# Layer 0's second shift computed as row sums on VectorE, with only the second scale left to TensorE

## The chip, the cores and the metric

The kernel runs on 1 core of one Trainium2 chip. A time is the device time of one execution in microseconds (us), lower is better. The core's engines are TensorE (PE in the rows; its weight loads are PEld), VectorE (DVE), ScalarE (ACT), GpSimd (POOL) and SyncE (SP), whose queue starts most DMA transfers. Each engine works through its own instructions in order.

## What is computed

Two layers of a hybrid diffusion backbone are applied to 128 context tokens and 256 latent tokens of width 1024. Each layer has a token-mixing half and a ConvFFN half, and both are modulated by six vectors that come from a conditioning vector. Cut to what matters here:

```python
def layer(x, mod, p, latent, kc, vc):
    sh1, sc1, g1, sh2, sc2, g2 = jnp.split(mod, 6)   # mod = silu(c) @ w_mod + b_mod
    h = layer_norm(x) * (1 + sc1) + sh1
    z = h @ p["w_in"] + p["b_in"]        # q, k, v, conv input, Fourier input, 3 gates
    ...                                  # attention, conv and Fourier branches
    merged = ga * a_attn + gc * a_conv + gf * a_f
    x = layer_norm(ALPHA * x + g1 * (merged @ p["w_o"]))
    h = layer_norm(x) * (1 + sc2) + sh2
    u = dwconv(h @ p["w_up"])
    ug, uv = jnp.split(u, 2)
    x = layer_norm(ALPHA * x + g2 * ((silu(ug) * uv) @ p["w_down"]))
```

There are two conditioning vectors (context and latent), so each of the six vectors exists twice. All inputs are float32.

## The kernel before

Tokens are kept transposed (`hT`: channels on the partitions, 384 tokens along the free axis). A float32 product is made of three matmuls (`mm3`, lines 197 to 200) on a high and a low half of each operand. For each weight tile `halves` (lines 171 to 183) has ScalarE cast the high half (`whi`, L181) and VectorE subtract it for the low half (`wlo`, L182). There are five buffers for each half.

The mixing half of a layer runs three branches one after the other, each over eight output tiles m of 128 channels (`branch`): branch 0 Fourier, branch 1 attention, branch 2 convolution. For a tile, TensorE makes a gate product of 24 matmuls into one of two `ps` accumulators, then the branch's own product into one of six `acc` accumulators (6 matmuls in branches 0 and 2, 12 in branch 1). ScalarE takes the tanh of the gate (L586), VectorE multiplies gate and product (L600), which frees the `acc` accumulator, and GpSimd adds the result to the running sum (L601). In branch 2 the finished sum is split into halves `r` (L569 on ScalarE, L570 on VectorE). Afterwards the output projection with `w_o` begins.

Beside that run, as generators that are stepped once per tile:

- attention: `scores` (softmax) and `values`, which transposes the probabilities and copies them out of the accumulators, 512 columns by ScalarE (L801) and 384 by VectorE (L802), before the products with V (L810, L813). There are 4 calls of `values` for a layer, with 2 copies of each kind.
- the depthwise convolution, 31 taps on VectorE (L828), whose results TensorE transposes (L836) for a layer norm.
- modulation by TensorE: `mod_stream` loads `w_mod` and multiplies it by the two conditioning vectors, which are padded to 32 columns (`cpad`). For each of 8 values of k, four matmuls on four quarters of the array (L219) cover 4 x 512 columns. They make layer 0's second shift and second scale in one go (kind "B"). `mod_columns` then copies the rows (L284), transposes them (L288) and adds the bias (L296).
- modulation by VectorE: `mod_rows` makes one of the six vectors (a unit) as row sums. For each of 8 tiles of `w_modr` (128x1024, two buffers) and each of the two conditioning vectors, one instruction multiplies and sums over 1024 columns (L318). In layer 0's mixing half it makes only the first gate, (0,"G",0). `paced(rows, n)` spreads the steps over n calls.
- `gate_rows`, right after the last tile of branch 2: TensorE transposes the gate's 16 sums (L338), ScalarE copies them and a DMA takes them to memory, from where they are broadcast.

A framework puts each engine's instructions into one fixed order when the program is built. The order is therefore not that of the source alone.

Of the kernel before, what the change touches and what calls it, by code (L numbers as in the profile page):

```python
# [13 lines left out]
ALU = mybir.AluOpType  # L14
AX = mybir.AxisListType

P = 128
D = 1024
KD = D // P
# [58 lines left out]
class Net:  # L78
# [130 lines left out]

    MODS = {"A": 0, "B": 1, "G": 2}  # L210

    STRIDE = 2

    def mod_products(self, ps, src, ks, n):

# [20 lines left out]
        self.mod_columns(l, "A", ps, P, 2 * s, "ps")  # L236
        yield

    def mod_stream(self, groups):


        steps = [(l, kind, k) for l, kind in groups for k in range(0, KD, self.STRIDE)]
        src = {}

        def fetch(l, kind, k0):
            for k in range(k0, k0 + self.STRIDE):
                w = self.a["w_mod"][l, self.MODS[kind], k].rearrange("p j (i c) -> p (j i) c", c=512)
                for i in range(4):
                    src[k, i] = self.s2()
                    self.load(src[k, i], w[:, i])  # L250

        fetch(*steps[0])
        yield
        for n, (l, kind, k0) in enumerate(steps):
            if k0 == 0:
                ps = self.psum("acc")
            self.mod_products(ps, src, range(k0, k0 + self.STRIDE), 512)
            if k0 + self.STRIDE == KD:
                if kind == "G":
                    self.mod_gates(l, ps)  # L260
                else:
                    self.mod_columns(l, kind, ps, 512, 0, "acc")
            if n + 1 < len(steps):
                fetch(*steps[n + 1])
            yield

    def mod_gates(self, l, ps):
        nc, a, n = self.nc, self.a, 512
        row = self.s2()
        nc.gpsimd.memset(row, 0.0)  # L270
        r4 = row.rearrange("(j i r) c -> j i r c", r=32, j=2)
        for v in range(2):
            for j in range(2):
                self.load(r4[j, :, v, :], a["b_g"][l, j].rearrange("(i c) -> i c", c=n))
        nc.vector.tensor_tensor(row, ps, row, op=ALU.add)
        for v in range(2):
            for j in range(2):
                nc.sync.dma_start(self.gscr[l, j, v].rearrange("(i c) -> i c", c=n), r4[j, :, v, :])

    def mod_columns(self, l, kind, ps, n, k0, tag):  # L280

# [259 lines left out]
    def mixing(self, l, first, hT, mods, rows):  # L541
        nc, a = self.nc, self.a
# [4 lines left out]
        def conv_in():  # L547
            gl = []
            for u in range(2):
                for j, w in enumerate(self.halves(self.col_halves(self.raw(a["w_cv"][l, u])))):  # L550
                    ps = self.ws_tile(hT, w)
                    gt = self.g()[:, 0:NTOK]
                    bias = cols["b_conv"][:, 2 * u + j:2 * u + j + 1]
                    if u == 0:
                        nc.scalar.activation(gt, ps, AF.Identity, bias=bias)
                    else:
                        nc.scalar.activation(gt, ps, AF.Tanh, bias=bias, scale=0.5)
                    gl.append(gt)
                    yield
            for j in range(2):  # L560
                for o, s, n in ((UP_S, 0, LAT), (UP_P, LAT, CTX)):
                    nc.vector.scalar_tensor_tensor(self.upad[j][:, o:o + n], gl[2 + j][:, s:s + n], 1.0,
                                                   gl[j][:, s:s + n], op0=ALU.add, op1=ALU.mult)
# [44 lines left out]

        if l + 1 < DEPTH:
            self.columns(l + 1)  # L610
        mods = self.mod_stream(mods) if mods else iter(())

        def mod():
            next(mods, None)

        step_rows = self.paced(rows, 10)
        ci = conv_in()
        next(ci)
        cv = self.keys(l, z)
# [20 lines left out]
                mod()  # L640
        for i, _ in enumerate(branch(1, 0, "w_a", 4, aT, lambda: values(3))):
            next(cb, None)
            if i >= 4:
                step_rows()
            if i % 2:
                mod()
# [84 lines left out]
    def attention(self, l, z, cv, out):  # L731
        nc, a = self.nc, self.a
# [57 lines left out]
        def values(j):  # L790
            pT = []
            for par in range(2):
                pr = prob.pop(2 * j + par)
                pts = [self.psum("acc"), self.psum("acc")]
                for i in range(3):
                    dst = pts[i // 2][:, (i % 2) * 256:(i % 2) * 256 + 256]
                    for t in range(2):
                        nc.tensor.transpose(dst[:, t * P:(t + 1) * P], pr[t][:, i * P:(i + 1) * P], self.ident)  # L798
                nc.tensor.transpose(pts[1][:, 256:384], pr[2], self.ident)
                p = self.s4()  # L800
                nc.scalar.copy(p[:, 0:512], pts[0])  # L801
                nc.vector.tensor_copy(p[:, 512:896], pts[1][:, 0:384])  # L802
                pT.append(p)
            po = self.psum("acc")
            vc = slice(j // 2 * HD, j // 2 * HD + HD)
            for i in range(4):
                for par in range(2):
                    pv = po[64 * par:64 * par + 64, :]
                    if i < 3:
                        nc.tensor.matmul(pv[:, 0:LAT], vs[i][:, vc], pT[par][:, i * 256:i * 256 + 256],  # L810
                                         start=i == 0, stop=i == 2)
                    else:
                        nc.tensor.matmul(pv[:, LAT:NTOK], vs[3][:, vc], pT[par][:, 768:896], start=True, stop=True)  # L813
            out.append(self.split_r(po[:, 0:NTOK]))
# [235 lines left out]
    def run(self):  # L1050
        self.setup()
        xhat = [self.s4() for _ in range(3)]
        for t in range(3):
            self.load(xhat[t], self.x_src(0, t))
        self.columns(0)
        for x in xhat:
            self.norm(x, x, D)
        mods = [[(0, "B")], []]
        mix_rows = [[(0, "G", 0)], [(1, "G", 0)]]
        ffn_rows = [[(0, "G", 1), (1, "A", 0), (1, "A", 1), (1, "B", 0), (1, "B", 1)], [(1, "G", 1)]]  # L1060
        first, hT = xhat, self.new_hT(0)
        for l in range(DEPTH):
            first, hT = self.layer(l, first, hT, mods[l], mix_rows[l], ffn_rows[l])
# [79 lines left out]
```

## Time and profile before

| | us |
|---|---|
| median of 3 runs (1138.2 to 1139.53) | 1138.48 |
| the profiled execution, its own time | 1139.04 |
| its span, from first to last instruction | 1137.3 |
| TensorE busy | 1115.4 |
| VectorE busy | 887.9 |
| ScalarE busy | 520.7 |

The profiled execution was 0.56 us above the median, and 1.74 us of its time lie outside the span. Times in the rows below count from the start of the span. Layer 0's three branches lie between about 90 and 256 us.

### The profile page before, as it was taken

The page shows a single profiled execution, that of the slowest core. Times are in us where ns is not written, and L with a number is a line of the kernel's source. Part 1 is how long each engine was busy: PE and PEld are TensorE (multiplying, and loading weights), DVE is VectorE, ACT ScalarE, POOL GpSimd, SP SyncE. Part 2 cuts the span into 40 slices and gives each one's busy share as a digit, 9 for nine tenths or more (in the row PEclk, how much of TensorE's full clock was granted, in tenths as well). Part 3 has the DMA queues.
Part 4 walks back from the last instruction along what each step waited for, and adds up shares of the span by engine and source line. Part 5 has one row for each costly group of instructions (what it writes and reads, how often), then busy time and mean ns, then how long its engine had stood idle before and what let it go on. Part 6 is the DMA issues. An engine that isn't in the chain of part 4 may idle for free.

```text
span 1137.3 us, 16435 instructions
## 1 busy us (share of the span) xinstructions
PE 1115.4 (98%) x6377; PEld 1013.8 (89%) x6377; DVE 887.9 (78%) x1529; ACT 520.7 (46%) x879; POOL 89.6 (8%) x89
## 2 busy tenths in 40 slices
PE   8999999999999999999999999999999999999996
PEld 6788889998999998999957989999889999999995
DVE  5579977855899999999776699796588975556668
ACT  2447653342753443444363686343356343444440
POOL 1010003221100000000021000222120000000001
PEclk9999999999999999999999999999999999999998
DMA  9753563636466666758324322564627543434511
GB/s 376 293 199 135 175 243 126 202 131 222 165 229 211 229 215 213 236 188 286 121 109 173 110 75 74 186 222 149 222 94 259 190 144 114 147 112 156 178 38 56
DMA packets 41822, 199.04 MB, mean 175 GB/s; under 512 B 4912, under 2 KB 6032, under 8 KB 26640
## 3 DMA queue, kind: packets, MB, share of 16 engines
q1 hardware_dynamic: 41312, 197.21, 49.7%
q8 instruction: 50, 0.82, 0.3%
q10 hardware_dynamic: 432, 0.79, 0.2%
q14 instruction: 28, 0.23, 0.1%
HBM read 194.53 MB, written 3.45 MB: 174 GB/s over the span
## 4 chain that ended last, share of the span: by engine, by line
PE 81%; DVE 10%; DMA 3%; ACT 3%; POOL 1%; issue 1%; SPq 0%; POOLq 0%; DVEq 0%; ACTq 0%
PE ps L198 16%; PE ps L200 16%; PE ps L199 16%; PE acc L199 9%; PE acc L200 9%; PE acc L198 9%; DVE s L318 1%; PE acc L810 1%; DVE wlo L182 1%; DMA s<-w_z 1%; DVE sm L404 1%; ACT whi L181 1%; DVE s L861 1%; POOL sm L408 1%; PE acc L798 1%
## 5 line engine op out<-in xcount | busy, mean ns | idle before, releaser
L182 DVE TENSOR_TENSOR wlo<-raw,whi 128x1024 fp32r<-128x1024 f32 x216 | 269.0, 1249 | 146.5 <-ACT whi L181 146.4
L198 PE MATMUL ps<-hT,whi 128*128 128x386 f32 (+1 forms) x1088 | 370.2, 340 | 2.4 <-ACT g L586 1.4
L181 ACT CAST whi<-raw 128x1024 fp32r<-128x1024 f32 x216 | 225.7, 1049 | 312.6 <-PE ps L199 185.6
L200 PE MATMUL ps<-hT,wlo 128*128 128x386 f32 (+1 forms) x1088 | 368.6, 339 | 0.0
L199 PE MATMUL ps<-hT,whi 128*128 128x386 f32 (+1 forms) x1088 | 368.5, 339 | 0.0
L198 PEld LDWEIGHTS ps<-hT,whi 128*128 128x128 f32 x1088 | 205.1, 189 | 9.4 <-issue 3.9
L199 PEld LDWEIGHTS ps<-hT,whi 128*128 128x128 f32 x1088 | 205.3, 189 | 1.5 <-issue 0.4
L200 PEld LDWEIGHTS ps<-hT,wlo 128*128 128x128 f32 x1088 | 205.2, 189 | 0.8 <-issue 0.7
L318 DVE SCALAR_TENSOR_TENSOR s<-s,s 128x1024 f32<-128x1024 f32 x128 | 160.6, 1255 | 4.4 <-DMA s<-w_modr 3.9
L199 PE MATMUL acc<-wlo,r 128*128 128x512 f32 x360 | 142.3, 395 | 1.0 <-DVE wlo L182 1.0
L200 PE MATMUL acc<-whi,r 128*128 128x512 f32 x360 | 141.9, 394 | 0.0
L198 PE MATMUL acc<-whi,r 128*128 128x512 f32 x360 | 140.3, 395 | 0.0
L200 PEld LDWEIGHTS acc<-whi,r 128*128 128x128 f32 x360 | 67.6, 188 | 15.9 <-DVE r L994 0.5
L199 PEld LDWEIGHTS acc<-wlo,r 128*128 128x128 f32 x360 | 67.6, 188 | 15.6 <-DVE wlo L182 1.3
L198 PEld LDWEIGHTS acc<-whi,r 128*128 128x128 f32 x360 | 67.6, 188 | 14.8
L408 POOL TENSOR_TENSOR sm<-sm,mhalf 128x1 f32<-128x1 f32 x21 | 26.8, 1274 | 617.5 <-DVE sm L407 616.8
L828 DVE SCALAR_TENSOR_TENSOR cv<-upad,cst,cv 128x399 f32<-128x399 f32 x120 | 70.6, 632 | 0.1
L601 POOL TENSOR_TENSOR g<-g,g 128x384 f32<-128x384 f32 x32 | 45.1, 1409 | 322.6 <-DVE g L600 322.6
L970 ACT ACTIVATE g<-ps,cst 128x386 f32<-128x386 f32 x84 | 56.1, 667 | 0.0
L971 DVE SCALAR_TENSOR_TENSOR g<-ps,cst,g 128x385 f32<-128x385 f32 x84 | 51.5, 613 | 2.5 <-ACT g L970 2.4
L973 DVE SCALAR_TENSOR_TENSOR g<-ps,cst,g 128x385 f32<-128x385 f32 x84 | 51.8, 617 | 1.3
L993 ACT CAST r<-g 128x386 fp32r<-128x386 f32 x44 | 22.6, 514 | 65.7 <-DVE g L991 65.7
(190 smaller groups left out, 1315.6 us busy)
## 6 DMA issues: line engine op xcount, KB each, us to landing
raw<-w_u SPq DMA_DIRECT2D x44, 1024.0 KB, 5.1
s<-w_modr SPq DMA_DIRECT2D x64, 512.0 KB, 3.8
raw<-w_g SPq DMA_DIRECT2D x24, 1024.0 KB, 5.0
raw<-w_d SPq DMA_DIRECT2D x22, 1024.0 KB, 4.9
raw<-w_mod SPq DMA_DIRECT2D x8, 1024.0 KB, 8.9
s<-w_mod SPq DMA_DIRECT2D x32, 256.0 KB, 4.8
raw<-w_o SPq DMA_DIRECT2D x8, 1024.0 KB, 4.9
s<-w_z SPq DMA_DIRECT2D x8, 512.0 KB, 9.3
```

The lines of the kernel that those rows point to most:

```text
L181: self.nc.scalar.copy(hi, raw)
L182: self.nc.vector.tensor_tensor(lo, raw, f32(hi), op=ALU.subtract)
L198: mm(ps, lh, rh, start=first, stop=False)
L199: mm(ps, lh, rl, start=False, stop=False)
L200: mm(ps, ll, rh, start=False, stop=last)
L318: nc.vector.scalar_tensor_tensor(prod, w[i % 2], 1.0, cb[v], op0=ALU.mult, op1=ALU.mult, accum_out=sums[n][:, v * KD + k:v * KD + k + 1])
L408: nc.gpsimd.tensor_tensor(mv[:, 3:4], mv[:, 2:3], self.mhalf, op=ALU.pow)
L601: nc.gpsimd.tensor_tensor(merged[m], merged[m], gt, op=ALU.add)
L828: nc.vector.scalar_tensor_tensor(c, u[:, i:i + CV_W], w, c, op0=ALU.mult, op1=ALU.add)
L970: nc.scalar.activation(c, ps, AF.Identity, bias=cols["ffn_b"][:, i:i + 1], scale=w[1])
L971: nc.vector.scalar_tensor_tensor(c[:, 1:NPAD], ps[:, 0:NPAD - 1], w[0], c[:, 1:NPAD], op0=ALU.mult, op1=ALU.add)
L973: nc.vector.scalar_tensor_tensor(c[:, 0:NPAD - 1], ps[:, 1:NPAD], w[2], c[:, 0:NPAD - 1], op0=ALU.mult, op1=ALU.add)
```

## The change

Layer 0's second shift, the unit (0,"B",0), moves to `mod_rows`. It is put ahead of the gate's unit, so that `mod_rows` has 17 steps instead of 9. `mod_stream` keeps the second scale alone: the same four quarters of the array now take 256 columns each, the transposes drop from four to two, and a fetch brings four values of k with two loads each. The steps of `mod_rows` are spread over 14 calls instead of 10 and may begin at tile 2 of branch 1 instead of tile 4. Besides, both copies in `values` go to ScalarE, in both layers.

```diff
-    STRIDE = 2
+    STRIDE = 4
...
-    def mod_stream(self, groups):
+    def mod_stream(self, l):
...
+                w = self.a["w_mod"][l, self.MODS["B"], k, :, 1]
+                for h in range(2):
+                    t = self.s2()
+                    self.load(t, w[:, h * 512:h * 512 + 512])
+                    for i in range(2):
+                        src[k, 2 * h + i] = t[:, i * 256:i * 256 + 256]
...
-            self.mod_products(ps, src, range(k0, k0 + self.STRIDE), 512)
+            self.mod_products(ps, src, range(k0, k0 + self.STRIDE), 256)
             if k0 + self.STRIDE == KD:
...
+                self.mod_column(l, 1, ps)
...
+    def mod_column(self, l, j, ps):
+
+        nc = self.nc
+        row = self.s2()[:, 0:256]
+        nc.vector.tensor_copy(row, ps[:, 0:256])
+        pt = self.psum("acc")
+        for q in range(2):
+            nc.tensor.transpose(pt[:, q * P:(q + 1) * P], row[:, q * P:(q + 1) * P], self.ident)
...
-        step_rows = self.paced(rows, 10)
+        step_rows = self.paced(rows, 14 if len(rows) > 1 else 10)
...
-            if i >= 4:
+            if i >= (2 if len(rows) > 1 else 4):
                 step_rows()
...
                 nc.scalar.copy(p[:, 0:512], pts[0])
-                nc.vector.tensor_copy(p[:, 512:896], pts[1][:, 0:384])
+                nc.scalar.copy(p[:, 512:896], pts[1][:, 0:384])
...
-        mods = [[(0, "B")], []]
-        mix_rows = [[(0, "G", 0)], [(1, "G", 0)]]
+        mods = [True, False]
+        mix_rows = [[(0, "B", 0), (0, "G", 0)], [(1, "G", 0)]]
```

In the changed file the lines behind the edit stand two lines higher: L318 becomes L316, L600 becomes L598, L570 becomes L568, L338 becomes L336. The three places that follow are where VectorE begins the row sums, where it ends them, and where TensorE takes the gate's sums.

VectorE, layer norm of the convolution in branch 1, before: the row sums (`s` and `sm` written) begin beside the third statistics.

```order
L413 TENSOR_SCALAR g_1998<-acc_1995,sm_2001 128x256
L407 TENSOR_SCALAR sm_2012<-sm_2012 128x1
L406 BN_AGGR sm_2023<-sm_2021 128x2
L318 SCALAR_TENSOR_TENSOR s_2162,sm_2165<-s_2163,s_2158 128x1024
L413 TENSOR_SCALAR g_2009<-acc_2006,sm_2012 128x256
```

The same place after the change:

```order
L405 TENSOR_SCALAR sm_1976<-sm_1976 128x1
L404 BN_AGGR sm_1987<-sm_1985 128x2
L316 SCALAR_TENSOR_TENSOR s_1996,sm_1999<-s_1997,s_1992 128x1024
L411 TENSOR_SCALAR g_1973<-acc_1970,sm_1976 128x256
L405 TENSOR_SCALAR sm_1987<-sm_1987 128x1
```

The first row sum has not moved to an earlier place: it still follows the third statistics, though two more tiles of branch 1 may call it.

VectorE near the end of branch 2, before; `g_2639` is the merge of tile 6 and `g_2679` that of tile 7:

```order
L182 TENSOR_TENSOR wlo_2766<-raw_2763,whi_2765 128x1024
L600 SCALAR_TENSOR_TENSOR g_2639<-g_2639,acc_2641 128x384
L570 SCALAR_TENSOR_TENSOR r_2651<-g_1542,r_2650 128x384
L941 MEMSET ps_2954 128x2
L455 CAST hT_2875<-zero_103 128x8x2
L455 CAST hT_2876<-zero_103 128x8x2
L182 TENSOR_TENSOR wlo_2770<-raw_2763,whi_2769 128x1024
L600 SCALAR_TENSOR_TENSOR g_2679<-g_2679,acc_2681 128x384
```

The same after; `g_2624` is the merge of tile 6, and `sm_2000` holds the gate's sums:

```order
L568 SCALAR_TENSOR_TENSOR r_2583<-g_1480,r_2582 128x384
L316 SCALAR_TENSOR_TENSOR s_1996,sm_2000<-s_1998,s_1992 128x1024
L182 TENSOR_TENSOR wlo_2715<-raw_2708,whi_2714 128x1024
L316 SCALAR_TENSOR_TENSOR s_1996,sm_2000<-s_1998,s_1994 128x1024
L326 TENSOR_TENSOR sm_2000<-sm_2000,cst_132 128x8
L182 TENSOR_TENSOR wlo_2757<-raw_2754,whi_2756 128x1024
L598 SCALAR_TENSOR_TENSOR g_2624<-g_2624,acc_2626 128x384
L568 SCALAR_TENSOR_TENSOR r_2636<-g_1549,r_2635 128x384
L326 TENSOR_TENSOR sm_2000<-sm_2000,cst_132 128x8
```

Before, the last row sum stood ahead of branch 2's first merge. Now the last one stands between the merges of tiles 5 and 6, and the gate's last bias addition behind the merge of tile 6.

TensorE at the end of branch 2, before:

```order
L200 MATMUL acc_2681<-r_2092,wlo_2330 128x384
L338 MATMUL acc_2698<-ident,sm_2165 16x128
L198 MATMUL acc_2711<-whi_2719,r_2408 128x512
L199 MATMUL acc_2711<-wlo_2720,r_2408 128x512
```

and after:

```order
L200 MATMUL acc_2668<-r_2070,wlo_2307 128x384
L336 MATMUL acc_2689<-ident,sm_2000 16x128
L198 MATMUL acc_2702<-whi_2710,r_2387 128x512
L199 MATMUL acc_2702<-wlo_2711,r_2387 128x512
```

Nothing moved here: the transpose of the gate's sums still stands directly between the last product of branch 2 and the first of `w_o`.

## Rows read from the trace of the kernel before

**Rows 1.** The page: engines (busy us, share, instructions), and the chain that ended last.

```profile
PE 1115.4 (98%) x6377; PEld 1013.8 (89%) x6377; DVE 887.9 (78%) x1529; ACT 520.7 (46%) x879; POOL 89.6 (8%) x89
...
PE 81%; DVE 10%; DMA 3%; ACT 3%; POOL 1%; issue 1%; SPq 0%; POOLq 0%; DVEq 0%; ACTq 0%
```

**Rows 2.** Busy by stretch: length, PE, PEld, DVE, ACT, POOL, clock, DMA share, GB/s.

```profile
160.00:182.00 22.00, 21.96 (x139) 20.66 (x138) 10.08 (x16) 7.08 (x10) 2.04 (x2) 1.00 0.64 238
182.00:224.00 42.00, 42.00 (x244) 41.82 (x243) 39.35 (x65) 15.34 (x21) 14.15 (x9) 1.00 0.52 176
224.00:256.00 32.00, 32.00 (x185) 32.00 (x184) 16.51 (x24) 13.94 (x21) 8.19 (x7) 1.00 0.39 132
```

**Rows 3.** Timeline of PE at modulation products: start, duration (each matmul is two records).

```profile
43.15 1.95 PE L219 MATMUL ps<-raw,cpad 128*32 128x128 f32 x64
...
139.81 1.06 PE L219 MATMUL acc<-s,cpad 128*32 128x512 f32 x8
140.80 0.87 PE L798 MATMUL acc<-ident,g 128*128 128x128 f32 x6
...
156.03 1.92 PE L219 MATMUL acc<-s,cpad 128*32 128x512 f32 x16
157.89 0.44 PE L198 MATMUL ps<-hT,whi 128*128 128x384 f32 x1
...
159.76 0.60 PE L288 MATMUL acc<-ident,s 128*128 128x128 f32 x4
160.11 0.42 PE L199 MATMUL ps<-hT,whi 128*128 128x384 f32 x1
```

**Rows 4.** Timeline of DVE at the copy of the modulation rows.

```profile
158.83 0.68 DVE L284 COPY s<-acc 128x512 f32<-128x512 f32 x1
```

**Rows 5.** Groups by line, 90 to 165 us: count, busy, mean ns, idle before.

```profile
L801 ACT COPY s<-acc 128x512 f32<-128x512 f32 x8 | 4.5, 579 | 1.5 <-PE acc L798 1.5
L802 DVE COPY s<-acc 128x384 f32<-128x384 f32 x7 | 3.9, 552 | 2.7 <-PE acc L799 2.6
```

**Rows 6.** Timeline of PE: transposes of the convolution, transpose of the gate's sums.

```profile
181.32 0.82 PE L836 MATMUL acc<-ident,cv 128*128 128x128 f32 x6
...
256.33 0.27 PE L338 MATMUL acc<-ident,sm 128*16 128x128 f32 x1
```

**Rows 7.** Timeline of DVE from the convolution's layer norm to the last row sum.

```profile
182.06 0.42 DVE L404 BATCH_NORM_STATS2 sm<-acc 128x6 f32<-128x256 f32 x1
...
206.35 2.04 DVE L318 SCALAR_TENSOR_TENSOR s<-s,s 128x1024 f32<-128x1024 f32 x1
...
208.43 1.22 DVE L318 SCALAR_TENSOR_TENSOR s<-s,s 128x1024 f32<-128x1024 f32 x1
...
209.70 1.23 DVE L318 SCALAR_TENSOR_TENSOR s<-s,s 128x1024 f32<-128x1024 f32 x1
...
210.85 1.22 DVE L182 TENSOR_TENSOR wlo<-raw,whi 128x1024 fp32r<-128x1024 f32 x1
211.99 0.55 DVE L600 SCALAR_TENSOR_TENSOR g<-g,acc 128x384 f32<-128x384 f32 x1
212.45 1.22 DVE L318 SCALAR_TENSOR_TENSOR s<-s,s 128x1024 f32<-128x1024 f32 x1
...
223.50 1.22 DVE L182 TENSOR_TENSOR wlo<-raw,whi 128x1024 fp32r<-128x1024 f32 x1
```

**Rows 8.** Group of the row sums by line, 182.06 to 223.59 us.

```profile
L318 DVE SCALAR_TENSOR_TENSOR s<-s,s 128x1024 f32<-128x1024 f32 x16 | 21.9, 1370 | 1.5 <-DMA s<-w_modr 1.4
```

**Rows 9.** Timeline of POOL: two additions to the running sum.

```profile
182.22 1.01 POOL L601 TENSOR_TENSOR g<-g,g 128x384 f32<-128x384 f32 x1 [5.28 <-DVE g L600]
...
205.38 1.93 POOL L601 TENSOR_TENSOR g<-g,g 128x384 f32<-128x384 f32 x1 [5.31 <-DVE g L600]
```

**Rows 10.** The transfers of `w_modr` tiles, 160 to 230 us.

```profile
DMA to landing us min/median/max: 3.4/4.2/8.0
```

More of the change, by code (lines that the diff above doesn't have):

```diff
@@ L237, in mod_first, with fetch @@
         yield
-    def mod_stream(self, groups):
-        steps = [(l, kind, k) for l, kind in groups for k in range(0, KD, self.STRIDE)]
+    def mod_stream(self, l):
         src = {}
-        def fetch(l, kind, k0):
+        def fetch(k0):
             for k in range(k0, k0 + self.STRIDE):
[L247 to L252, printed above, removed]
+                w = self.a["w_mod"][l, self.MODS["B"], k, :, 1]
[4 more added lines that the diff above has]
+                        src[k, 2 * h + i] = t[:, i * 256:i * 256 + 256]
+        fetch(0)
@@ L253, in mod_stream @@
         yield
-        for n, (l, kind, k0) in enumerate(steps):
+        for k0 in range(0, KD, self.STRIDE):
             if k0 == 0:
                 ps = self.psum("acc")
-            self.mod_products(ps, src, range(k0, k0 + self.STRIDE), 512)
+            self.mod_products(ps, src, range(k0, k0 + self.STRIDE), 256)
             if k0 + self.STRIDE == KD:
[L259 to L264, printed above, removed]
-            yield
@@ L267, in mod_gates @@
[L267 to L271, printed above, removed]
-        for v in range(2):
[L273 to L278, printed above, removed]
+                self.mod_column(l, 1, ps)
+            else:
+                fetch(k0 + self.STRIDE)
@@ new lines, in mod_stream @@
+            yield
+    def mod_column(self, l, j, ps):
[5 more added lines that the diff above has]
+            nc.tensor.transpose(pt[:, q * P:(q + 1) * P], row[:, q * P:(q + 1) * P], self.ident)
+        bias = self.bmod[l][:, j + 3, :].rearrange("p (i q) -> p i q", q=2)
+        for v in range(2):
+            part = pt[:, 0:256].rearrange("p (q i r) -> p r i q", q=2, i=4)[:, v]
+            dst = self.modcol[l][:, j + 2, v, :].rearrange("p (i q) -> p i q", q=2)
+            nc.vector.tensor_tensor(dst, part, bias, op=ALU.add)
@@ L610, in mixing @@
             self.columns(l + 1)
-        mods = self.mod_stream(mods) if mods else iter(())
+        mods = self.mod_stream(l) if mods else iter(())
         def mod():
             next(mods, None)
-        step_rows = self.paced(rows, 10)
+        step_rows = self.paced(rows, 14 if len(rows) > 1 else 10)
         ci = conv_in()
```

## The prediction

> **What bounds the kernel now.** I read the page first. TensorE is busy for 98% of the span and carries 81% of the chain that ended last, while VectorE is busy for 78% [rows 1]. So an instruction that leaves TensorE is worth its own time, and work added to VectorE costs nothing as long as TensorE never has to wait for it. Whether it will have to is a question for the stage in which the work is put, and so I went on to busy time by stretch [rows 2]. In layer 0, TensorE is busy without a gap in all three stretches. VectorE is not: it has 11.9 us free from 160 to 182 us, only 2.65 us from 182 to 224 us, where the 16 row sums of the gate stand, and 15.5 us from 224 to 256 us. The reader should see that VectorE is already full in the middle stretch. Then I read the two timelines there, and the order of the instructions.
>
> **What TensorE is relieved of.** The products of `mod_stream` stand in six stretches, four with one value of k and two with two values. One value lasts 0.99 us from its start to the start of the next work (139.81 to 140.80), two last 1.86 us (156.03 to 157.89) [rows 3]. That is 4 x 0.99 + 2 x 1.86 = 7.7 us for eight values. The trace has no such product with 256 columns. It has it with 128: 64 records, eight values of k, in 1.95 us, or 0.24 us each [rows 3]. The two ends are thus 0.24 us (no dearer than 128 columns) and 0.93 us (no cheaper than 512), which would save 5.8 or 0.3 us. The two rows lie nearly on a line through zero (four times the columns, 3.9 times the price), so I take the value on that line, 0.24 + (0.93 - 0.24)/3 = 0.47 us. Eight of them cost 3.8 us and save 3.9 us. Of four transposes (0.35 us, 159.76 to 160.11 [rows 3]) two go, 0.2 us. TensorE is relieved of **4.1 us**.
>
> **What attention pays.** Sixteen copies of 384 columns (0.55 us each) go from VectorE to ScalarE, over two layers. There they queue beside the copies of 512 columns (0.58 us), so that the second copy of a pair comes later instead of at the same time [rows 5]. The products with V wait for it. At best the matmuls that stand between hide it, price 0; at worst each of the 8 calls of `values` loses one copy, 8 x 0.55 = 4.4 us. Two things lie on this path too. The modulation products, whose stretches filled the time in which TensorE waited for copies, are shorter now. And the copy in `mod_column` has fewer matmuls ahead of its transposes (one of a gate product and four of attention). Before, that copy began 0.94 us after the products' end (157.89 to 158.83 [rows 3, 4]). In most of the calls the new order has matmuls of a gate product in between, so I stay near the lower end: **1.0 us** for all of it. VectorE's gain of 16 copies is worth nothing by itself, since TensorE did not wait for it there.
>
> **What the row sums cost.** This is the term that decides. The sixteen added row sums are not placed earlier: the first still follows the convolution's layer norm, for which TensorE makes the transposes at 181.32 us [rows 6]. The free 11.9 us from 160 to 182 us are of no use to them. The deadline is the transpose of the gate's sums, which TensorE has directly behind the last product of branch 2 and reaches at 256.33 us, 75.0 us after those transposes [rows 6]. The number of matmuls in between is the same in both orders. Now I follow VectorE along its new order.
>
> First half: from the first statistics at 182.06 us to the end of the first unit. The instructions are of the same kinds and numbers as those of before up to 223.50 us (16 row sums, 8 `wlo` splits, 5 merges, the norms), so they take the same 41.4 us [rows 7].
>
> Second half: from there to the gate's last bias addition, which replaces the relaxed stretch of 224 to 256 us. Start to start, a row sum takes 1.27 us when another follows (208.43 to 209.70) and 1.15 us otherwise (209.70 to 210.85), a split 1.14 us, a merge 0.46 us [rows 7]. I count an `r` like a merge. The order has 5 x 1.27 + 11 x 1.15 = 19.0 us of row sums, 8 splits with 9.1 us, 7 merges and 6 `r` with 6.0 us, and two bias additions with 0.2 us, together 34.3 us. Six of the row sums come right behind a merge (or behind the `r` that follows it), just when GpSimd adds to the running sum. Then a row sum takes 2.04 us instead of 1.22 [rows 7], and the addition 1.93 us instead of 1.01 [rows 9]. Six times 0.82 is 4.9 us, and the half takes 39.2 us.
>
> VectorE is therefore through at 182.06 + 41.4 + 39.2 = 262.7 us on the old clock, and TensorE, in order, stands at 256.33 us and waits **6.4 us**. As a second look: the added 19.0 and 4.9 us exceed the 18.2 us that VectorE had free from 182 to 256 us by 5.7 us [rows 2]. From below, without any collision in the second half, the wait is 1.5 us. From above: a tile of `w_modr` lands in 4.2 us, but also in 8.0 us [rows 10], and such waits already took 1.4 us for eight tiles [rows 8]. One late tile in the second half adds 3.8 us, and the wait is 10.2 us. I take 6.4 us because the collision shows at the row sums behind merges in branch 1.
>
> The Trainium skill has a rule for this collision that speaks against the change. "SBUF — State Buffer", section Who interferes with whom, says that a VectorE instruction with two inputs in SBUF contends with a GpSimd instruction that reads SBUF, and that the later of the two is blocked until the first is over. The trace agrees (1.93 instead of 1.01 us for the addition). By the rule each of the six row sums could lose up to a whole addition of 1.01 us, which would make 6.1 us of the 4.9 and a wait of 7.6 us.
>
> Nothing later takes the wait back. The output projection that follows is as dense on TensorE as what stands ahead of it. On the way, two smaller waits start in branch 2: the tanh of a gate stands behind the `r` of the tile before on ScalarE, which waits for GpSimd, which waits for the merge, and there are only two `ps` accumulators. What they cost TensorE is spent from the same 6.4 us, because VectorE's own row of work is not made longer by it. The weights' halves and the first sums of `w_o` are ready in time.
>
> **Sum.** -4.1 + 1.0 + 6.4 = +3.3 us on the profiled execution's 1139.04 us. On the median of 1138.48 us that is 1141.8 us. One measurement of this kernel can tell about 0.2% (2.3 us) from no change, so this is just outside.
>
> **The rivals.** *VectorE keeps pace.* If the row sums slip into the free 15.5 us of the last stretch and the wait is nil, there remains 1138.48 - 4.1 + 1.0 = 1135.4 us, faster than before. For it speaks that the stretch 224 to 256 us was half empty. Against it speaks that the added work exceeds all free time from 182 us on. It decides if VectorE's second half takes under 32.9 us (256.33 - 182.06 - 41.4) instead of 39.2. *Half a wait.* GpSimd's additions find a split or an `r` instead of a row sum, and the wait is 1.5 to 4 us: 1136.9 to 1139.4 us, no change that can be told. For it speaks that not every overlap needs to be a whole one. *Late tiles.* The two `w_modr` buffers are refilled just in time, with 4.2 us for a landing and about 4.5 us between two uses of a buffer where a split and two merges lie between them (1.27 + 1.15 + 1.14 + 2 x 0.46 us). With one landing of 8.0 us or more, or with attention at its upper end, it is about 1146 us. *The quarters are not halved.* If 256 columns cost what 512 do, 3.8 us of the relief are gone: 1145.6 us. The two measured widths speak against it.
>
> **How the numbers follow.** I give the forecast 0.45 (1140.8 to 1144.5 us), half a wait 0.22, keeping pace 0.15, late tiles or dear copies 0.13, and the unhalved products 0.05. The two ends of all terms are 1138.48 - 4.1 + 0 + 1.5 = 1135.9 and 1138.48 - 4.1 + 4.4 + 10.2 = 1149.0 us. A range from 1135.4 to 1147.0 us leaves out about half of the faster case and the far end of the slow ones, some 1 in 10 together. Faster by over 0.2% comes from keeping pace alone: 0.15. Slower: 0.45 less a little for its lower edge, with 0.18 from the two slow rivals, 0.60. Within 0.2%: 0.25.
>
> **What would show it.** Right: TensorE waits several microseconds for VectorE at the transpose of the gate's sums (L336), VectorE is busy nearly without a gap from the convolution's norm to there, row sums of about 2.0 us follow the merges in branch 2, and the eight products sum to about 3.8 us. Wrong: TensorE passes from branch 2 to `w_o` without a wait, or VectorE idles in branch 2 for tiles of `w_modr` or for ScalarE. If TensorE waits at the products with V, the attention term was too small.

## The result and the profile after

The changed kernel takes 1145.38 us (median of 4 runs, 1144.77 to 1146.48), the kernel before 1138.85 us in the same comparison. The ratio is 1.0055 (95% interval 1.0043 to 1.0067): slower by 6.5 us. The profiled execution took 1146.48 us with a span of 1144.7 us, 7.4 us longer than the span before. One execution below, the profiled one of gate_first, took 2828 us against 1143.19 to 1146.28 us of its other four, and its trace is not read.

The page's engines (busy us, share, instructions) and the chain that ended last answer to [rows 1]:

```profile
PE 1117.6 (98%) x6375; PEld 1016.5 (89%) x6375; DVE 903.1 (79%) x1545; ACT 526.2 (46%) x895; POOL 88.6 (8%) x89
...
PE 76%; DVE 14%; ACT 3%; DMA 3%; issue 3%; POOL 2%; POOLq 0%; DVEq 0%; SPq 0%; ACTq 0%
```

VectorE's share of the chain rose from 10 to 14%, and TensorE's fell from 81 to 76%. The busy times by stretch, as in [rows 2], show where:

```profile
160.00:182.00 22.00, 22.00 (x133) 20.45 (x132) 11.12 (x20) 7.63 (x12) 3.55 (x4) 1.00 0.66 239
182.00:224.00 42.00, 42.00 (x244) 41.81 (x243) 39.88 (x60) 15.35 (x21) 11.72 (x7) 1.00 0.61 201
224.00:256.00 32.00, 30.87 (x172) 29.56 (x170) 31.83 (x45) 11.86 (x18) 7.87 (x6) 1.00 0.59 197
256.00:262.00 6.00, 0.79 (x3) 0.69 (x4) 5.33 (x11) 1.57 (x4) 1.18 (x1) 0.75 0.53 175
```

The third busy time of a line is VectorE's: free for 15.5 us from 224 to 256 us before, it is now full there (31.83 of 32 us). From 256 to 262 us TensorE works for only 0.79 of 6 us. The waits of TensorE from 85 to 300 us (total, times, longest):

```profile
PE acc L336 <- DVE ps L939: 5.3, 1, 5.3
PE ps L198 <- ACT g L584: 1.8, 3, 0.8
```

Of the three waits for a tanh (L584), one of 0.7 us stands in branch 0, at 103.02 us, as in the kernel before; the other two are in branch 2. The MEMSET at L939 is only the last VectorE instruction ahead of the transpose. What the transpose of the gate's sums (L336) needs is the bias addition in front of it, which VectorE's timeline shows with the last two row sums:

```profile
247.35 2.04 DVE L316 SCALAR_TENSOR_TENSOR s<-s,s 128x1024 f32<-128x1024 f32 x1
...
253.80 2.04 DVE L316 SCALAR_TENSOR_TENSOR s<-s,s 128x1024 f32<-128x1024 f32 x1
...
256.92 1.21 DVE L316 SCALAR_TENSOR_TENSOR s<-s,s 128x1024 f32<-128x1024 f32 x1
...
260.21 0.95 DVE L326 TENSOR_TENSOR sm<-sm,cst 128x8 f32<-128x8 f32 x1
```

TensorE by stretch behind its last matmul of branch 2 (length, PE, granted clock, DMA share, GB/s):

```profile
255.90:261.20 5.30, 0.03 (x1) 0.79 0.58 192
...
262.00:263.00 1.00, 1.00 (x4) 0.50 0.00 0
263.00:264.00 1.00, 1.00 (x4) 0.50 0.00 0
264.00:265.00 1.00, 1.00 (x4) 0.50 0.33 41
265.00:266.00 1.00, 1.00 (x5) 0.57 0.76 188
266.00:267.00 1.00, 1.00 (x6) 1.00 0.93 393
```

After the standstill TensorE goes on at the lower of its two levels, 1.2 GHz (0.50), until about 265.7 us: 0.43 us from one matmul of 128x512 to the next (261.82 to 265.66 us, nine of them) instead of 0.235.

Three marks cut the program into stages: the start of the convolution's transposes in layer 0, the start of the gate's transpose, and the start of the same gate's transpose in the ConvFFN half. From the groups of their lines (first and last start):

```profile
L834 PE MATMUL acc<-ident,cv x12: 271/273/273, 178.9 to 739.7; 128*128 128x128 f32 x12
...
L336 PE MATMUL acc<-ident,sm x2: 270/326/381, 261.2 to 814.2; 128*16 128x128 f32 x2
```

The stage from the first mark to the second takes 82.3 us (261.21 - 178.91), against 75.0 us before [rows 6]. The next one, to 501.54 us, takes 240.33 us, against 237.97 (256.33 to 494.30). All later stages agree with those before within 0.3 us. The stage ahead, from the last product of the first modulation (begun at 45.3 us, before at 44.8) to the first mark, takes 133.6 us instead of 136.5. So the sum is -2.9 + 7.3 + 2.4 = +6.8 us; the other 0.6 us of the span are mostly the start (0.5).

### The profile page after: what moved, and what is told of

Its sections match the earlier page's. It is cut to its first block, busy times and chain, and to the rows that moved or that the text cites. A ratio compares the mean times of both kernels' runs of the same rounds, so it can differ in the third digit from the quotient of the medians.

```text
span 1144.7 us, 16452 instructions
## 1 busy us (share of the span) xinstructions
PE 1117.6 (98%) x6375; PEld 1016.5 (89%) x6375; DVE 903.1 (79%) x1545; ACT 526.2 (46%) x895; POOL 88.6 (8%) x89
## 4 chain that ended last, share of the span: by engine, by line
PE 76%; DVE 14%; ACT 3%; DMA 3%; issue 3%; POOL 2%; POOLq 0%; DVEq 0%; SPq 0%; ACTq 0%
PE ps L198 15%; PE ps L199 15%; PE ps L200 14%; PE acc L198 8%; PE acc L199 8%; PE acc L200 8%; DVE s L316 3%; DVE wlo L182 2%; DMA s<-w_modr 1%; PE acc L808 1%; DVE sm L402 1%; ACT whi L181 1%; POOL sm L406 1%; DVE s L869 1%; PE acc L796 1%
## 5 line engine op out<-in xcount | busy, mean ns | idle before, releaser
L316 DVE SCALAR_TENSOR_TENSOR s<-s,s 128x1024 f32<-128x1024 f32 x144 | 183.4, 1273 | 3.8 <-DMA s<-w_modr 3.0
```

The costliest lines, as they stand in the source:

```text
L316: nc.vector.scalar_tensor_tensor(prod, w[i % 2], 1.0, cb[v], op0=ALU.mult, op1=ALU.mult, accum_out=sums[n][:, v * KD + k:v * KD + k + 1])
```

## The experiments

Every kernel ran beside the kernel before on the same chip; the ratios are to it (its median was 1138.85 to 1139.25 us). The two stage columns are read from one trace of each kernel as above. The execution behind a trace lay up to 2.5 us from its kernel's median (the change 1146.48, `filler` 1147.66, `early` 1139.54, `late_two_cb` 1139.24 us), so they say where time went, and the medians how much.

| kernel | median us | ratio (95% interval) | conv. to gate transpose | to the ConvFFN's |
|---|---|---|---|---|
| before | 1138.85 | | 75.0 | 238.0 |
| the change | 1145.38 | 1.0055 (1.0043 to 1.0067) | 82.3 | 240.3 |
| no_sums | 1135.39 | 0.9967 (0.9954 to 0.9979) | 75.0 | 238.3 |
| copies_only | 1139.63 | 1.0007 (0.9998 to 1.0015) | 75.0 | 238.7 |
| copies_back | 1144.84 | 1.0045 (1.0032 to 1.0058) | 82.3 | 239.9 |
| no_adds | 1139.39 | 1.0008 (0.9998 to 1.0017) | 77.7 | 238.2 |
| gate_first | 1144.17 | 1.0045 (1.0031 to 1.0058) | | |
| gate_first_2 | 1144.60 | 1.0050 (1.0038 to 1.0063) | 76.8 | 245.8 |
| filler | 1145.16 | 1.0053 (1.0041 to 1.0066) | 82.3 | 240.9 |
| filler_ps | 1147.04 | 1.0062 (1.0048 to 1.0076) | 81.8 | 241.1 |
| early | 1141.28 | 1.0022 (1.0013 to 1.0031) | 77.2 | 240.1 |
| late_two | 1140.52 | 1.0008 (1.0000 to 1.0017) | 78.1 | 240.2 |
| late_two_cb | 1141.63 | 1.0016 (1.0006 to 1.0025) | 76.9 | 241.0 |
| late_pinned | 1157.50 | 1.0163 (1.0150 to 1.0176) | 76.7 | 258.4 |

**no_sums: the change without the sixteen row sums.**

```diff
-        mix_rows = [[(0, "B", 0), (0, "G", 0)], [(1, "G", 0)]]
+        mix_rows = [[(0, "G", 0)], [(1, "G", 0)]]
...
+                for v in range(2):
+                    self.nc.vector.tensor_copy(self.modcol[l][:, 2, v, :], self.bmod[l][:, 3, :])
```

> The sixteen row sums of the second shift are left out, so that this shift is its bias alone; the second scale's quarters, the copies on ScalarE and the rest of the change stay. Theory (the row sums cost 5.5 us of wait, 1.7 us of small waits and 2.3 us of clock; all else together saves about 3 us): 1145.4 - 9.5 = 1135.9 us, faster than before by 2.6 us. Rival (the copies on ScalarE eat the relief of TensorE): 1138 to 1139 us.

The kernel leaves out the loads of the shift's eight `w_modr` tiles together with the row sums. 1135.39 us: the theory. The first stage is back at 75.0 us. The whole loss hangs on the row sums and their loads, 1145.38 - 1135.39 = 10.0 us, and all the rest of the change together gains 3.8 us (1139.22 us for the kernel before in that job).

**gate_first: the gate's unit ahead of the shift's.**

```diff
-        mix_rows = [[(0, "B", 0), (0, "G", 0)], [(1, "G", 0)]]
+        mix_rows = [[(0, "G", 0), (0, "B", 0)], [(1, "G", 0)]]
```

> The two units of the row sums change places: the gate's sums come first, the second shift's last. VectorE has the same instructions. Theory (TensorE stands 5.5 us at the transpose of the gate's sums because VectorE makes them last, and then runs 4.7 us at clock 0.50, which costs 2.3 us): both are gone, 1145.4 - 5.5 - 2.3 = 1137.6 us, and the small waits for a tanh in branch 2 stay. Rival (VectorE is too full whatever stands last, so the wait only moves to the first splits of w_o): 1143 to 1145 us, with a wait of TensorE for wlo instead.

1144.17 us, so the theory fell: the gate's sums were not the reason by themselves. The rival had the time right. The kernel was run again for a trace that can be read.

> The kernel with the gate's unit first once more, for its trace. Theory (the transpose of the gate's sums is only the first thing that comes late; the output projection needs all six acc accumulators, and these are freed by the last merge on VectorE and by ScalarE's copy of the transposed sums, which stands behind the r casts): no wait at the transpose, but one of 3 us or more in the first 12 us of w_o, on the last merge, the copy or the r casts, at 1143 to 1145 us. Rival (TensorE waits for the wlo splits of w_o, which stand behind the last row sums): a wait of the same size for wlo.

The waits of TensorE in that trace, from 176 to 300 us:

```profile
PE acc L198 <- ACT kk L338: 2.5, 1, 2.5
PE acc L198 <- DVE g L598: 1.7, 1, 1.7
PE ps L198 <- ACT g L584: 1.2, 2, 0.8
```

There is no wait at the gate's transpose, and none for `wlo`, which the rivals named; instead of one wait of 3 us there are two. The output projection opens with six accumulators, which are all there are, and TensorE waits for the fourth until VectorE has made a late merge (L598), and then for the fifth until ScalarE has copied the transposed sums (L338), which stands behind the casts of the late `r`. Behind these two waits the clock falls as well:

```profile
259.00:262.60 3.60, 0.97 (x3) 0.49 (x3) 2.27 (x7) 2.09 (x5) 1.19 (x1) 0.69 0.39 164
262.60:266.00 3.40, 3.36 (x8) 2.64 (x9) 3.40 (x4) 1.81 (x3) 1.18 (x1) 0.50 0.53 140
```

So the theory became: VectorE is late with everything at the end of branch 2, and the transpose is only the first to feel it.

**no_adds: no additions by GpSimd in layer 0's branch 2.** Only branch 2 reaches the output projection.

```diff
-                        nc.gpsimd.tensor_tensor(merged[m], merged[m], gt, op=ALU.add)
+                        if l == 0 and br == 2:
+                            merged[m] = gt
+                        else:
+                            nc.gpsimd.tensor_tensor(merged[m], merged[m], gt, op=ALU.add)
```

> In layer 0's branch 2 GpSimd's addition to the running sum is left out, so that only branch 2 reaches the output projection; VectorE keeps every instruction, its row sums among them. Theory (the collision with these additions costs six row sums 0.82 us each, and the r cast that waits for the addition holds up the tanh): VectorE is through 4.9 us sooner, no row sum of branch 2 takes 2.0 us, the small waits for a tanh go, and with them most of the wait and of the low clock: 1136.5 to 1139 us. Rival (the row sums cost what they cost, collision or not, and VectorE is too full anyway): 1143 us or more.

1139.39 us, 0.4 us above the theory's range and far from the rival. The groups of the row sums on VectorE show why; first the changed kernel (222 to 261 us), then this one (222 to 257 us), count, busy us, mean ns:

```profile
L316 DVE SCALAR_TENSOR_TENSOR s<-s,s 128x1024 f32<-128x1024 f32 x16 | 24.3, 1518 | 0.2
```

```profile
L316 DVE SCALAR_TENSOR_TENSOR s<-s,s 128x1024 f32<-128x1024 f32 x15 | 18.3, 1220 | 1.4 <-DMA s<-w_modr 1.2
```

Sixteen times 1518 - 1220 ns is 4.8 us for the collision. A wait remains at the transpose, but the clock stays up through it:

```profile
PE acc L336 <- DVE sm L326: 2.6, 1, 2.6
```

```profile
254.00:256.50 2.50, 0.01 (x1) 0.00 (x0) 2.50 (x8) 0.49 (x2) 0.00 (x0) 1.00 0.91 279
```

**filler and filler_ps: matmuls in place of the wait.** Twenty-nine matmuls of 128x384 that nothing reads, ahead of the transpose; in the second kernel they and the transpose use a `ps` accumulator.

```diff
+            for _ in range(fill):
+                nc.tensor.matmul(pt[:, 0:NTOK], r[:, 0:P], r, start=True, stop=True)
```

> TensorE gets 29 matmuls of 128x384 that nothing uses, directly ahead of the transpose of the gate's sums, 29 x 0.17 = 5.0 us of added work in the place of the wait. Theory (2.3 us of the loss are the half clock that follows the idle time, not the wait itself): the transpose still starts at the same moment, the clock stays at 1.00 and the time falls to 1145.4 - 2.3 = 1143.1 us. Rival (the clock falls for another reason, or the lower clock costs nothing): 1145.4 us or, if the matmuls delay something, more.

> The filling matmuls once more, but they and the transpose write a ps accumulator, so that no acc accumulator of w_o waits for ScalarE's copy of the transposed sums. Theory (29 matmuls keep the clock at 1.00, which is worth 2.3 us; in the first such run 1.5 to 2 us of it were eaten by the wait for that copy): 1143 to 1144 us, below the changed kernel, no wait of over 0.5 us behind the transpose. Rival (the clock is not what the time hangs on there, since w_o would wait for the last merge anyway): 1145 us or more.

The clock does stay at 1.00, in both. But nothing is gained: 1145.16 and 1147.04 us, the rivals' times within 0.3 us. In the first, TensorE at full clock runs into the wait for ScalarE's copy (TensorE by stretch, and its waits):

```profile
266.00:268.00 2.00, 0.93 (x5) 1.00 0.73 303
```

```profile
PE acc L198 <- ACT kk L341: 1.1, 1, 1.1
```

In the second that wait is gone, and w_o runs without a gap from 260 to 268 us, so it did not wait for the last merge either, as the rival has it. Yet VectorE then waits for the residual stream, whose load was issued 10.8 us behind the transpose (270.53 us) instead of 7.2 before (263.54), and the transposes behind w_o come late. Here are VectorE's wait and these transposes, in filler_ps and then in the kernel before:

```profile
DVE s L862 <- DMA s<-x_s: 3.3, 1, 3.3
```

```profile
290.69 1.09 PE L434 MATMUL acc<-ident,s 128*128 128x128 f32 x8 [0.78 <-ACT s L425]
```

```profile
286.39 1.04 PE L433 MATMUL acc<-ident,s 128*128 128x128 f32 x8
```

Counted from the gate's transpose they start after 30.06 us before, 32.14 in the changed kernel, 31.76 in filler and 31.00 in filler_ps. So up to there filler_ps does win back 1.1 of the changed kernel's 2.1 us, and loses them again in the ConvFFN half: of its 3.1 us in that stage only 0.9 come with this load, and the other 2.2 are not explained. Nor is the median, which lies 2.3 us above the profiled execution (1144.73). The theory that the clock's 2.3 us can be had back did not hold in these two kernels; since in filler_ps the transpose also takes a `ps` accumulator out of its turn, they do not show that the clock has no price.

**early: row sums from tile 0 of branch 1 on.**

```diff
-        step_rows = self.paced(rows, 14 if len(rows) > 1 else 10)
+        step_rows = self.paced(rows, 16 if len(rows) > 1 else 10)
...
-            if i >= (2 if len(rows) > 1 else 4):
+            if i >= (0 if len(rows) > 1 else 4):
```

> The row sums may begin at tile 0 of branch 1 instead of tile 2 (16 slots instead of 14), so that about five of them stand ahead of the convolution's layer norm on VectorE, in the time in which it had 11 us free. Theory (the work is not too much, only too late): VectorE is through some 6 us sooner, the wait at the gate's transpose is gone with its lower clock, 1145.4 - 5.5 - 2.3 - up to 1.7 = 1136 to 1138 us. Rival (TensorE's wait moves to the norm of the convolution or to merges, which now stand behind row sums): 1140 us or more.

1141.28 us: the rival. The wait at the transpose is gone, and two others stand there, one at each end (waits of TensorE, 176 to 300 us):

```profile
PE acc L198 <- ACT kk L338: 1.6, 1, 1.6
PE acc L842 <- DVE g L411: 1.6, 2, 1.2
```

The second is the convolution's layer norm, which now stands behind row sums. The first is ScalarE's copy of the transposed sums, as in gate_first_2.

**late_pinned: the gate first, ten row sums behind VectorE's last merge.** `mixing` hands `step_rows` on, with 17 slots from tile 4, and the loop over w_o steps it.

```diff
+                with self.tc.issue_after(self.last_merge.ins):
+                    step_rows()
```

> The gate's unit comes first, as in the kernel before, and about ten of the shift's sixteen row sums are moved behind VectorE's last merge, into the output projection, where VectorE was busy for 5.7 us out of 14. Everything else of the change stays. Theory (the row sums are affordable where no accumulator waits behind them): no wait of TensorE at the gate's transpose nor at the start of w_o, and the time is near that without the row sums, 1135.4 to 1137 us, faster than before by 2 to 4 us. Rival (the late row sums hold up the splits of w_o or the layer norm behind it, or the shift itself comes late for the ConvFFN): 1139 us or more, with a wait of TensorE between 260 and 290 us.

1157.50 us: the rival, and far above its lower bound. TensorE reached the transpose 76.7 us after the first mark, and lost 20 us in the stage behind it. VectorE's waits from 256 to 300 us, and TensorE's from 256 to 312 us:

```profile
DVE s L316 <- DMA s<-w_modr: 7.1, 2, 6.3
```

```profile
PE acc L431 <- ACT s L422: 8.0, 1, 8.0
```

The DMA engines are 86 to 97% busy from 260 to 276 us, with `w_u` beside the tiles. The last tile of `w_modr` was issued only at 275.52 us, after SyncE's queue had waited 3.3 us for a row sum begun at 273.84 us, and it took 5.8 us to land, where the median in the changed kernel is 3.7. VectorE began on it at 281.39 us. Its free time in w_o was real, but with two buffers each tile's load waits for earlier row sums, and the next row sums wait for the load.

**late_two: the gate first, only the last two tiles behind the last merge** (the same edit with 16 slots from tile 2, so that both tiles are fetched during branch 2), and **late_two_cb**, with the copies back on VectorE.

> The gate's unit first, and only the last two tiles of the shift (four row sums), whose weights are fetched while branch 2 still runs, stand behind VectorE's last merge; everything else as in the change. Theory (what hurts is the work ahead of VectorE's last merges, and the late version failed on a tile that was fetched late, not on the place): the last merge comes some 5 us sooner, no wait at the gate's transpose nor at the start of w_o above 0.5 us, no low clock; the small waits for a tanh stay: 1136 to 1138 us, faster than before. Rival (row sums in w_o are bad as such, because the layer norm behind it stands behind them): 1140 us or more, with a wait between 270 and 300 us.

> The same, with the 384-column copies of attention back on VectorE. The run with the copies alone came out 0.6 us slower than before with an interval that touches zero. Theory (the copies cost about 0.6 us): 0.3 to 0.9 us below the other kernel. Rival (VectorE, with 16 copies more, reaches the convolution's norm later and gives it back): equal or above.

1140.52 and 1141.63 us, so the theory missed again; the rival had the time right, but TensorE has no wait between 270 and 300 us. The low clock and the long waits are gone, but the short ones stay (late_two, 178 to 300 us):

```profile
PE ps L198 <- ACT g L584: 2.0, 3, 0.9
PE acc L198 <- ACT kk L338: 1.4, 1, 1.4
```

The second of them is again ScalarE's copy behind the `r` casts, and with it the transposes behind w_o come 2.1 us later than before (32.16 us behind the gate's instead of 30.06). So late_two is 5 us better than the change and no better than before.

**copies_only and copies_back: the copies of attention.** The first is the kernel before with the copy on ScalarE, the second the changed kernel with it back on VectorE.

```diff
-                nc.vector.tensor_copy(p[:, 512:896], pts[1][:, 0:384])
+                nc.scalar.copy(p[:, 512:896], pts[1][:, 0:384])
```

> The kernel before with the one edit that the 384-column copies of attention go to ScalarE, in both layers. Theory of the prediction: attention pays 1.0 us, so 1.0 us above the kernel before of the same job. Rival 1 (the copies are hidden behind matmuls that stand between): within 0.4 us of it. Rival 2 (each call of values loses a copy): 4.4 us above it.

> The changed kernel with the 384-column copies of attention back on VectorE. Theory (in the changed kernel the copies cost what they cost alone): 0.3 to 0.9 us below the changed kernel's 1145.4, 1144.5 to 1145.1 us. Rival (VectorE, which is the late engine, has 8 copies more in this layer): above 1145.4 us.

1139.63 us (0.6 us above the 1138.99 us of its job, with an interval that reaches zero) and 1144.84 us (0.5 us below the change). In late_two_cb the same edit came out 1.1 us above. Over both layers the price lies between nothing and about 1 us. The traces tell more of layer 0. The stage ahead of the convolution's transposes, 136.5 us before, takes 138.4 us in copies_only (from 44.4 to 182.79 us), but 133.8 us in copies_back (45.4 to 179.16 us) against 133.6 us in the changed kernel; late_two and late_two_cb, which differ by the same edit, have 133.8 us both. So in these traces (one of each kernel) the copies cost nothing in this stage of the changed kernel.

## Why the prediction came out as it did

The forecast was 1141.8 us, slower, with a range up to 1147.0 us; 1145.38 us lies inside it and 3.6 us above the forecast. The band that the forecast itself was given, 1140.8 to 1144.5 us, is missed by 0.9 us. That the time is still inside the range is luck: its upper part stood there for late tiles, dear copies and products that are not halved, and none of the three happened (VectorE idled 0.2 us for its row sums from 222 to 261 us).

**TensorE's relief: right.** The stretches of products, each with the start of the work behind it:

```profile
106.28 0.64 PE L219 MATMUL acc<-s,cpad 128*32 128x256 f32 x8
106.85 0.86 PE L808 MATMUL acc<-s,s 128*64 128x256 f32 x5
...
107.86 1.50 PE L219 MATMUL acc<-s,cpad 128*32 128x256 f32 x24
109.30 0.43 PE L808 MATMUL acc<-s,col 128*64 128x256 f32 x1
```

One value of k lasts 0.57 us and three last 1.44; with the other two stretches (1.44 and 0.57) the eight take 4.0 us, against the 3.8 us of the line between 128 and 512 columns. The quarters are halved. With attention's price the stage was to gain 4.1 - 1.0 = 3.1 us and gained 2.9. That the sum is right is partly luck: with the copies back on VectorE the stage gains no more (2.7 us), so what took about 1 us of the relief was not the copies. What it was, no run shows.

**The wait: right in place and kind, a little small.** VectorE's chain from the convolution's first statistics (179.65 us) to the gate's bias addition (261.16 us) lasts 81.5 us; the sum was 41.4 + 39.2 = 80.6. The six collisions are there in branch 2, five at 2.03 to 2.04 us and one at 1.92, and no_adds prices them at 4.8 us, where 4.9 was reckoned. The last bias addition collides too, 0.95 us instead of 0.15, which is nearly all that the sum was short of. TensorE lost 7.3 us in the stage (82.3 - 75.0): 5.5 us at the transpose, since the last matmul of branch 2, begun at 255.59 us, is through by 255.76, and nearly all the rest in branch 2, where the gates' accumulators came free late. 6.4 us was forecast, so the term was 0.9 us short. That the small waits would be "spent from the same 6.4 us" held: VectorE's chain was not longer for them.

The Trainium skill, "SBUF — State Buffer", section Who interferes with whom, has the later of two such instructions blocked until the first is over. The trace agrees: GpSimd's addition that began at 247.10 us, beside an `r` of VectorE begun at 246.88 us, lasted 1.20 us instead of 1.01, and the row sum that began at 247.35 us ended 1.09 us behind it, nearly its undisturbed 1.22 us.

**"Nothing later takes the wait back" and "The weights' halves and the first sums of `w_o` are ready in time": here the prediction failed.** The first sentence is true as it stands, but by the two the prediction took the stage behind the transpose for neutral and gave it no term. The stage lost 2.4 us, most of it in the trace as half clock behind 5.5 us of standstill: ten matmuls of `w_o` from 261.25 to 265.66 us took 4.4 us, where the first takes 0.31 us at full clock and nine more 0.235 us each, 2.4 in all. These 2.0 us are a term for TensorE's clock, which the prediction does not have. In the changed kernel `w_o` then runs without a gap, but with TensorE 5.5 us late. Where TensorE came without that wait (gate_first_2) or at full clock (filler, filler_ps), it met what stands behind: a merge, a copy on ScalarE, a load. In five kernels in which either the wait at the transpose or the low clock was taken away (gate_first_2, filler, filler_ps, early, late_two) at least 2 us of loss remained in the stage behind it. Only without the row sums or without GpSimd's additions (no_sums, no_adds) was that stage back at 238.2 to 238.3 us.

**The sum.** The missing 2.4 us, the 0.9 us of the wait and 0.2 us of the relief are 3.5 of the 3.6 us. (They are read from the profiled executions, which differ by 7.4 us where the medians differ by 6.5; most of what is left there lies in the start.) The rival "keeping pace" needed VectorE's second half in 32.9 us; from the shift's last bias addition (begun at 221.15 us) to the gate's it took 40.0 us, so neither this rival nor half a wait came about.

## What to carry to other kernels

Work that is moved to an engine with free time must fit into the free time between its own release and the first thing that waits for it; here 16 row sums with 19 us, and nearly 5 more by collision, met 15.5 us, and the mean share of 78% said nothing of it. When an engine is late at the end of a stage, look for everything that it, the engines behind it and the load queue hand over to the next stage, not only for the first wait: taking away the wait at the transpose bought about 1 us of 10 as long as the work ahead of VectorE's last merges stayed (gate_first). And count what a standstill of TensorE does to the matmuls after it, but don't book it as a gain of its own until a kernel without it has been timed.

## What the runs showed of the hardware

TensorE's granted clock fell to 0.50 behind 5.5 us of standstill and stayed there for about 4.5 us of dense work. It fell too behind two waits of 1.9 and 2.6 us that only three matmuls parted (gate_first_2), and it stayed at 1.00 through 2.7 us of standstill in no_adds. The Trainium skill, "TensorE: Matmul & The Clock Gate", section What's actually happening, tells of such a gate that halves the array's clock after idleness; the changed kernel agrees (0.50), and no_adds shows an idle stretch without it.

A 128x8 addition on VectorE took 0.95 us instead of 0.15 beside a GpSimd addition: here the collision cost a small instruction as much (0.80 us) as a large one (0.82).
